# Queueing the S5 powers and matrices on VectorE behind the row norm of the second half of c

## The chip, the cores and the metric

The kernel runs on one core of a Trainium2 chip. The core has five engines that run side by side, each with its own queue that is worked through in order: TensorE (PE in the profile: matrix products and transposes), VectorE (DVE), ScalarE (ACT), GpSimd (POOL) and SyncE (SP, which issues the transfers here). An instruction that waits for another engine holds up all that is queued behind it on its own engine. The metric is the device time of one execution in microseconds (us).

## The reference

One layer on 1024 tokens of width 1024, all in float32: a layer norm, then a mixer of two branches, then a cross-attention and an MLP, each with its own residual and layer norm. The change lies in the first part of the mixer:

```python
z = h @ w_in                       # u 256 | c_q 256 | c_kv 256 | k_r 32 | gate 2048
y = s5_ssm(u, ...)                 # a diagonal complex state space, 16 groups of 64 states
q = rms_norm(c_q, q_norm_g) @ w_uq
kv = rms_norm(c_kv, kv_norm_g) @ w_ukv
```

`s5_ssm` forms a step factor a = exp(lam * dt) for every state, a factor f, and the scaled input matrix f * b; then it scans h(t) = a h(t-1) + b u(t) along the tokens and reads out with c. `rms_norm` divides each row of 256 by its root mean square.

## The kernel before, in words

**Tiles.** Token t of the input is c * 8 + s with s from 0 to 7; a tile of 128 rows holds one s. h0, the normed input, is kept feature-major as a pair of tiles, a rounded high part and a remainder; every large product is three TensorE passes (`mm3`, L147 to L152): high times high, high times low, low times high. Weights are split in the same way by `split_w` (L110 to L123): a transfer, a ScalarE cast (L120) and a GpSimd subtraction (L122).

**c.** `c_gemm(hf)` (L580 to L611) computes c_q and c_kv side by side for four row tiles (one half of the tokens) into two double PSUM banks. ScalarE copies the four results out (L596) and forms the sums of squares of each half row (L600). VectorE scales them and adds the epsilon (L602); `rsqrt` (L163 to L167) takes a VectorE reciprocal (L163), a ScalarE square root (L164), and three VectorE steps that refine it (L165 to L167). Then the rows are scaled: c_q by ScalarE (L610), c_kv by VectorE (L608). `c_T(hf, tl, ks)` turns one 128-column block k of the four tiles: `to_feature` has four TensorE transposes (L232) into a PSUM bank, the reading of that bank by ScalarE (L242) or, for the odd k, by VectorE too (L240), and a subtraction (L245) on VectorE, or on GpSimd for k = 2. The half 0 is computed first (`ct0`), the half 1 (`ct1`) has the four turns of half 0 as filling between its products.

**u.** The loop at L689 computes u and k_r for each s (24 passes of 288 columns into a PSUM bank), which ScalarE copies out (L699), and VectorE the 32 columns of k_r (L701). Before s = 3, 4, 5 and 6 one turn of ct1 is done.

**S5 on VectorE.** Between ct0 and ct1 stands the S5 preparation: the tables of sine and cosine and the exponentials (`exp_small`, `sincos`, L434 to L499), and then, from L649, the powers 0 to 8 of the step factor (L651 to L654, and three rounds of complex products in `cmul`, L503 to L508, at L671), the factor f (L656 to L668) and the scaled input matrix (L680). All of these are small: 8 to 128 columns. Behind the u loop stand the matrices of eight steps: G (L714 to L719) and O (L721 to L726), each 1024 columns wide, and the negated c (L728).

**What follows.** `gs_gemm(0)` and `gs_gemm(1)` (L733 to L741) are two long gate products; then TensorE turns G (L749) and takes the small products of G with c (L759, L760) between the passes of `gs_gemm(2)`. VectorE adds the skip (L772), turns k_r by its angles (L796 to L799), and the scan begins (from L831). O is first read at L887.

**Order.** The text of the kernel is not the order of the queues. A planner takes all instructions with their dependencies, plays the program through with costs of its own, and fills each engine's queue; of the instructions that are ready for an engine, the one that was written first goes first. So the place in the text acts as a priority, and something written far below can go ahead when nothing written above it is ready by the planner's clock. PSUM has four single banks (tag `ps1`) and two double ones here; the "x" tiles that hold c, u, G and O are eight.

## Time and profile before

| | us |
|---|---|
| median of 3 runs | 1653.34 |
| lowest and highest | 1650.19 and 1653.36 |
| profiled execution | 1652.23 |
| its span in the trace | 1650.4 |
| TensorE busy | 1539.5 (93%) |
| VectorE busy | 1243.3 (75%) |
| ScalarE busy | 976.5 (59%) |
| GpSimd busy | 988.0 (60%) |

The profile shows one execution. In a view in order of time each row has the start, the duration, the engine, the line of the kernel, the operation, the tiles it writes and reads with their shapes, the count, and in square brackets how long the engine was idle before it and what released it. Rows of neighbours overlap by some 0.07 us, since one instruction starts while the last is draining. In a view of waits each row has who waited for whom, the total, the count and the longest. In a view by windows the columns are the window, its length, the busy time (and instructions) of PE, PE's weight loads, DVE, ACT and POOL, the mean granted TensorE clock (1.00 is full), the share of the transfer engines, and GB/s.

### The profile page before, as it was taken

Reading aid. Unit: us, or ns where it says so; the run is one execution under the profiler, and the core shown is the slowest. Engines: PE = TensorE matmul, PEld = TensorE weight load, DVE = VectorE, ACT = ScalarE, POOL = GpSimd, SP = SyncE. Lnnn points to the kernel's source line nnn. Section 1 sums busy time; section 2 is a strip of 40 time slices with the busy share of each in tenths; the row PEclk is TensorE's granted clock in tenths of the full one; section 3 lists DMA queues with packets and bytes.
Section 4 is the critical chain, followed back from the end, with each engine's and each line's share of the span. In section 5 each row is a group of like instructions: output and inputs, shape, how many; then the busy total and the mean of one; then the engine's idle time right before and its main releaser. Section 6 shows DMA issues by size and latency. Waiting matters only on the chain.

```text
span 1650.4 us, 20758 instructions
## 1 busy us (share of the span) xinstructions
PE 1539.5 (93%) x7480; PEld 1263.0 (77%) x7480; DVE 1243.3 (75%) x1977; ACT 976.5 (59%) x1415; POOL 988.0 (60%) x538
## 2 busy tenths in 40 slices
PE   6979999999989999999977899899999999999995
PEld 4867778778768778778866687678888888888884
DVE  7970926767777969956574686999598949876998
ACT  5632235666678537684573647766866766667661
POOL 3223243664547767665563554676878767878776
PEclk9989999999999999999998899999999999999998
DMA  6212121111052541103220120022111302021102
GB/s 240 81 39 71 53 71 56 59 60 50 15 177 81 201 154 51 52 0 129 102 102 1 32 86 37 28 75 64 39 51 52 102 1 77 26 103 50 57 22 102
DMA packets 40107, 117.61 MB, mean 71 GB/s; under 512 B 4804, under 2 KB 6340, under 8 KB 40004
## 3 DMA queue, kind: packets, MB, share of 16 engines
q1 hardware_dynamic: 40004, 116.29, 20.5%
q8 instruction: 59, 0.97, 0.2%
q14 instruction: 44, 0.36, 0.1%
HBM read 98.90 MB, written 16.78 MB: 70 GB/s over the span
## 4 chain that ended last, share of the span: by engine, by line
PE 71%; DVE 15%; ACT 7%; POOL 3%; issue 3%; DMA 1%; SPq 0%; POOLq 0%; ACTq 0%; DVEq 0%
PE b L151 20%; PE b L150 20%; PE b L152 20%; DVE sx L1192 1%; PE bb L1034 1%; PE b L1071 1%; DVE c L182 1%; DVE t L371 1%; PE bb L1037 1%; DVE sx L1223 1%; ACT bb L367 1%; PE bb L1038 1%; PE b L1090 1%; DVE sx L224 1%; DVE sa L1249 1%
## 5 line engine op out<-in xcount | busy, mean ns | idle before, releaser
L151 PE MATMUL b<-sw,sa 128*128 128x512 f32 (+3 forms) x1504 | 579.6, 385 | 12.8 <-POOL sw L375 6.7
L150 PE MATMUL b<-sw,sa 128*128 128x512 f32 (+3 forms) x1504 | 578.6, 385 | 12.8 <-ACT sw L120 5.4
L152 PE MATMUL b<-sw,sa 128*128 128x512 f32 (+3 forms) x1504 | 577.7, 384 | 2.7 <-POOL sa L375 2.2
L151 PEld LDWEIGHTS b<-sw,sa 128*128 128x128 f32 x1504 | 284.7, 189 | 71.8 <-POOL sw L375 10.3
L150 PEld LDWEIGHTS b<-sw,sa 128*128 128x128 f32 x1504 | 284.5, 189 | 69.2 <-ACT sw L120 5.7
L152 PEld LDWEIGHTS b<-sw,sa 128*128 128x128 f32 x1504 | 284.5, 189 | 57.9 <-POOL sa L375 4.0
L375 POOL TENSOR_TENSOR sa<-t,sa 128x1024 fp32r<-128x1024 f32 x105 | 257.6, 2469 | 118.8 <-ACT sa L373 106.9
L367 ACT COPY bb<-sa 128x1024 f32<-128x1024 f32 x230 | 233.1, 1018 | 135.8 <-DVE t L371 69.1
L1192 DVE TENSOR_TENSOR sx<-sx,b 128x512 f32<-128x512 f32 x288 | 185.1, 675 | 35.2 <-PE b L152 35.0
L375 POOL TENSOR_TENSOR sw<-t,sw 128x1024 fp32r<-128x1024 f32 x73 | 180.9, 2484 | 43.4 <-ACT sw L373 34.2
L371 DVE TENSOR_TENSOR t<-bb,sa 128x1024 f32<-128x1024 f32 x119 | 144.1, 1217 | 35.1 <-ACT bb L367 18.9
L1249 DVE TENSOR_TENSOR sa<-sa,b 128x512 f32<-128x512 f32 x192 | 124.9, 678 | 46.8 <-ACT sa L1247 33.7
L373 ACT CAST sa<-t 128x1024 fp32r<-128x1024 f32 x105 | 109.1, 1049 | 59.3 <-DVE t L371 58.9
L362 POOL TENSOR_TENSOR sa<-sa,sa 128x1024 fp32r<-128x1024 f32 x36 | 90.2, 2519 | 57.8 <-ACT sa L361 34.2
L122 POOL TENSOR_TENSOR sw<-sraw,sw 128x1024 fp32r<-128x1024 f32 (+4 forms) x28 | 61.9, 2219 | 87.4 <-ACT sw L120 81.8
L150 PE MATMUL b<-sa,sw 128*128 128x512 f32 (+1 forms) x272 | 101.5, 373 | 3.3 <-DVE sa L1249 3.3
L152 PE MATMUL b<-sa,sw 128*128 128x512 f32 (+1 forms) x272 | 99.2, 365 | 0.0
L151 PE MATMUL b<-sa,sw 128*128 128x512 f32 (+1 forms) x272 | 99.2, 365 | 0.0
L362 POOL TENSOR_TENSOR sw<-sa,sw 128x1024 fp32r<-128x1024 f32 x32 | 81.1, 2550 | 27.9 <-ACT sw L361 27.9
L371 DVE TENSOR_TENSOR t<-bb,sraw 128x1024 f32<-128x1024 f32 x53 | 64.2, 1217 | 33.8 <-POOL sw L375 17.8
L373 ACT CAST sw<-t 128x1024 fp32r<-128x1024 f32 x73 | 76.2, 1052 | 15.3 <-PE b L151 7.6
L375 DVE TENSOR_TENSOR sw<-bb,sw 128x1024 fp32r<-128x1024 f32 x47 | 57.2, 1217 | 5.6 <-ACT sw L373 5.5
(341 smaller groups left out, 2792.5 us busy)
## 6 DMA issues: line engine op xcount, KB each, us to landing
sa<-in_w_up_dram SPq DMA_DIRECT2D x24, 512.0 KB, 4.0
sa<-in_w_dn_dram SPq DMA_DIRECT2D x24, 512.0 KB, 4.3
sx<-in_x_dram SPq DMA_DIRECT2D x16, 512.0 KB, 5.8
d_h<-t SPq DMA_DIRECT2D x16, 256.0 KB, 2.3
sraw<-in_w_gs_dram SPq DMA_DIRECT2D x8, 512.0 KB, 3.2
d_gs<-t SPq DMA_DIRECT2D x16, 256.0 KB, 2.9
t<-d_gs SPq DMA_DIRECT2D x16, 256.0 KB, 2.8
d_ms<-t SPq DMA_DIRECT2D x16, 256.0 KB, 2.1
```

The costliest lines, as they stand in the source:

```text
L122: (nc.vector if self.rawtag == "a" and self.nsw % SWV == 0 else nc.gpsimd).tensor_sub(lo[:, :cols].bitcast(FR), raw[:, :cols], hi[:, :cols])
L150: mm(out, A[0].bitcast(FR), B[0].bitcast(FR), start=start, stop=False)
L151: mm(out, A[0].bitcast(FR), B[1].bitcast(FR), start=False, stop=False)
L152: mm(out, A[1].bitcast(FR), B[0].bitcast(FR), start=False, stop=stop)
L182: self.nc.vector.bn_stats(st[:, h, :], x[:, h * 512:(h + 1) * 512])
L362: (GP if z is x[c] else V).tensor_sub(H[c][1].bitcast(FR), z, H[c][0])
L367: A.copy(P[c], x[c])
L371: V.tensor_tensor(T[c], P[c], y[c], op=op)
L373: A.copy(H[c][0].bitcast(FR), T[c])
L375: (V if T[c] is P[c] else GP).tensor_sub(H[c][1].bitcast(FR), T[c], H[c][0])
L1192: V.tensor_tensor(v, v, b, op=op)
L1249: V.tensor_tensor(z[:, s_], z[:, s_], b, op=op)
```

## The change

The text of `ct1 = c_gemm(1, ...)` and of the whole u loop is moved up: ahead of the powers instead of behind the scaled input matrix. `c_gemm` keeps the last of its VectorE row scalings (L608) in `k_.last_ts`. And all that stands from the powers to the negated c is put into a block, `tc.issue_after(ct1_last)`, which gives each VectorE instruction of the block an edge to that last scaling: the planner may queue it only behind it. The edge is one of order in VectorE's queue; it adds no wait between engines. Instructions of other engines, and VectorE's sine, cosine and exponentials ahead of the block, get no edge. The order in which tiles are asked for stays the same.

```diff
@@ c_gemm
-                    V.tensor_scalar(z, z, y[:, 2 * t + i:2 * t + i + 1], None, op0=ALU.mult)
+                    k_.last_ts = V.tensor_scalar(z, z, y[:, 2 * t + i:2 * t + i + 1], None, op0=ALU.mult)
@@ body, behind sincos
+    ct1 = c_gemm(1, [lambda k=k: c_T(0, ct0, (k,)) for k in range(4)])
+    ct1_last = k_.last_ts.ins
+    Uc = [k_.slot("x"), k_.slot("x")]
+    krx = k_.slot("x")
+    V.memset(krx[:, 0:768], 0.0)
...
+    for s in range(8):
+        if 2 < s < 7:
+            c_T(1, ct1, (s - 3,))
...
+        V.tensor_copy(krw[:, s, :], b[:, 256:288])
+
+    g_ = tc.issue_after(ct1_last)
+    g_.__enter__()
 
     apr = s5t(9)
     api = s5t(9)
...
     k_.cmul(V, bbr, bbi, frb, fib, br, bi, bt_)
-    ct1 = c_gemm(1, [lambda k=k: c_T(0, ct0, (k,)) for k in range(4)])
-    Uc = [k_.slot("x"), k_.slot("x")]
...
-        V.tensor_copy(krw[:, s, :], b[:, 256:288])
-
     Or, Oi, Gr, Gi = (k_.slot("x") for _ in range(4))
...
     V.tensor_scalar(nci, ci, -1.0, None, op0=ALU.mult)
+    g_.__exit__(None, None, None)
```

## The prediction

> **What bounds the kernel now.** I read first the page's busy shares and its chain of work that ended last, then the list of what TensorE waited for, then the order of time on TensorE, ScalarE and VectorE around one of its longest waits.

> ```profile
> PE 1539.5 (93%) x7480; PEld 1263.0 (77%) x7480; DVE 1243.3 (75%) x1977; ACT 976.5 (59%) x1415; POOL 988.0 (60%) x538
> PE 71%; DVE 15%; ACT 7%; POOL 3%; issue 3%; DMA 1%; SPq 0%; POOLq 0%; ACTq 0%; DVEq 0%
> ...
> PE b L150 <- ACT sa L1411: 11.8, 4, 7.1
> ...
> PE b L232 <- ACT sx L610: 10.2, 1, 10.2
> ...
> PE b L150 <- ACT sw L361: 4.1, 1, 4.1
> ```

> TensorE is the bound: it is idle for 1650.4 - 1539.5 = 110.9 us in all. 10.2 us of that are one wait, for the scaling L610 of c, and this is the place that the change is about. TensorE's order of time there:

> ```profile
> 83.67 0.29 PE L152 MATMUL b<-sw,sa 128*128 128x288 f32 x1
> 94.22 1.67 PE L232 MATMUL b<-cst,sx 128*128 128x128 f32 x4 [10.25 <-ACT sx L610]
> 95.54 0.59 PE L150 MATMUL b<-sw,sa 128*128 128x288 f32 x1
> 95.93 0.44 PE L151 MATMUL b<-sw,sa 128*128 128x288 f32 x1
> ...
> 100.01 0.34 PE L150 MATMUL b<-sw,sa 128*128 128x288 f32 x1
> ```

> TensorE has done three of the eight u products (83.97), then wants to transpose the normed second half of c, gets it at 94.22 and comes to the fourth u product at 95.54: 11.57 us later than its own queue would have had it, transposes included. ScalarE and VectorE say why:

> ```profile
> 80.48 0.19 ACT L600 ACTIVATION_READ_ACCUMULATOR t<-sx 128x1 f32 x1
> 80.87 1.06 ACT L120 CAST sw<-sraw 128x1024 fp32r<-128x1024 f32 x1
> 90.97 0.21 ACT L164 ACTIVATE c<-c 128x8 f32<-128x8 f32 x1 [9.04 <-DVE c L163]
> 93.65 1.71 ACT L610 ACTIVATE sx<-sx,c 128x256 f32<-128x256 f32 x4 [2.15 <-DVE c L167]
> ```

> ```profile
> 77.99 0.43 DVE L497 TENSOR_TENSOR sa<-sa,sx 128x264 f32<-128x264 f32 x1
> 78.41 1.25 DVE L245 TENSOR_TENSOR sa<-t,sa 128x512 fp32r<-128x512 f32 x1
> 82.10 2.38 DVE L508 TENSOR_TENSOR sa<-sa,sx 128x16 f32<-128x16 f32 x1
> 84.40 0.21 DVE L955 TENSOR_SCALAR sa<-sa 128x128 f32<-128x128 f32 x1
> 85.04 0.74 DVE L240 TENSOR_SCALAR t<-b,c 128x512 f32<-128x512 f32 x1
> 86.11 1.07 DVE L245 TENSOR_TENSOR sa<-t,sa 128x512 fp32r<-128x512 f32 x1
> 88.42 0.70 DVE L686 MEMSET sx<- 128x768 f32 x1
> 89.55 0.16 DVE L602 TENSOR_SCALAR c<-c 128x8 f32<-128x8 f32 x1
> 89.62 1.21 DVE L714 TENSOR_TENSOR sx<-sa,sx 128x1024 f32<-128x1024 f32 x1
> 93.45 0.17 DVE L167 SCALAR_TENSOR_TENSOR c<-c,c 128x8 f32<-128x8 f32 x1
> 94.67 1.13 DVE L608 TENSOR_SCALAR sx<-sx,c 128x256 f32<-128x256 f32 x4
> ```

> The sums of squares are in at 80.67. The next step of the norm, L602 on VectorE, starts at 89.55, because VectorE's queue has S5 work ahead of it. From L602 to L610 it is another 93.65 - 89.55 = 4.10 us for five tiny VectorE steps (L602, L163, L165 to L167) and a tiny one of ScalarE (L164), because a 1024-column S5 product (L714 and the like, 1.21 us) stands between each two.

> **The change part by part.** (a) The work moved behind L608 is 41 small operations (L651 to L680), twelve 1024-column ones (L714 to L726) and L728; all are VectorE's, and no DMA and no other engine's instruction moves. What stays ahead of L602 once TensorE's half is in: sine and cosine up to L497 (78.42), then those that are ahead of it today and don't belong to S5: L245 1.25, L240 0.74, L245 1.07, L686 0.70 and L955 twice 0.21, some 4.2 us less their small overlaps. So L602 could start at about 82.1, by 7.4 us sooner. The earliest is 80.75, when the squares are in, if the planner lets L602 pass them.

> (b) From L602 to L610 without the S5 products: the six tiny steps are some 0.17 us each (L602 0.16, L164 0.21, L167 0.17) with a hand-over between, for which I take 1.5 us in place of 4.10. Bounds: 1.0 (their bare durations, with nothing between) and 4.1 (other copies slip between).

> (c) A collision comes with it. The 16-column L508 above took 2.38 us, where L508 on 32 columns takes 0.18; it ended with a GpSimd subtraction that began just before it:

> ```profile
> 82.06 2.38 POOL L122 TENSOR_TENSOR sw<-sraw,sw 128x1024 fp32r<-128x1024 f32 x1 [10.16 <-ACT sw L120]
> 86.01 0.18 DVE L508 TENSOR_TENSOR sa<-sa,sx 128x32 f32<-128x32 f32 x1
> ```

> Today an S5 operation waits there; after the change it is the norm, or what stands just ahead of it, that is held until 84.44. With L602 or L163 held, L610 comes at 82.1 + 1.5 + 2.1 = 85.7; without the collision at 83.6. I take 85.7, since the norm's steps lie in the middle of that subtraction. [...]

> L610 at 85.7 in place of 93.65 is 7.95 us. TensorE's transposes and the fourth u product hang on L610 by 0.57 and 1.89 us, so that product starts at 87.6, and TensorE still idles some 2.3 us behind 83.97.

> (d) The clock. After the gap the u products start 0.24 us apart (95.93 to 100.01 in 17 steps); the granted clock in windows:

> ```profile
> 84.00:86.00 2.00, 0.00 (x0) 0.00 (x0) 2.00 (x9) 0.00 (x0) 0.45 (x1) 1.00 0.26 63
> 86.00:88.00 2.00, 0.00 (x0) 0.00 (x0) 2.00 (x4) 0.00 (x0) 0.00 (x0) 0.61 0.53 199
> 98.00:100.00 2.00, 2.00 (x10) 2.00 (x9) 1.87 (x2) 0.00 (x0) 0.00 (x0) 0.50 0.00 0
> 102.00:104.00 2.00, 2.00 (x17) 2.00 (x17) 1.19 (x2) 0.74 (x1) 0.00 (x0) 1.00 0.00 0
> 164.00:166.00 2.00, 0.31 (x4) 0.10 (x3) 1.95 (x7) 0.99 (x3) 1.47 (x2) 1.00 0.00 0
> 490.00:492.00 2.00, 2.00 (x6) 1.52 (x6) 1.72 (x2) 1.63 (x3) 0.00 (x0) 0.50 0.98 346
> ```

> At the half clock half of the 95.93 to 100.01 is lost, 2.0 us. The clock fell within 2.5 us of the start of the gap (it is 0.61 over 86 to 88); after the wait of 4.1 us for L361, at 488, it stands at 0.50 too, and it held around 165, where TensorE was idle for most of two us. A remaining gap of 2.3 us lies between, so I count 1.5 us of the 2.0 as gained; the bounds are 0 and 2.0. [...]

> (e) What the moved work costs in its new place. Its cover is TensorE's way from the fourth u product to the transposes L749 of the matrices G, its first reader:

> ```profile
> 114.89 0.40 PE L150 MATMUL b<-sa,sw 128*128 128x512 f32 x1
> 136.70 2.26 PE L749 MATMUL b<-cst,sx 128*128 128x128 f32 x16
> ...
> 95.90:119.00 23.10, 23.10 (x150) 22.37 (x150) 15.82 (x18) 10.03 (x18) 6.49 (x3) 0.91 0.02 4
> 119.00:160.00 41.00, 40.86 (x198) 30.98 (x196) 0.45 (x1) 9.15 (x13) 14.12 (x11) 1.00 0.28 95
> ```

> TensorE idles 0.14 us from 95.9 to 160, while VectorE is busy for 16.3 of those 64 us. After the change L749 would come at about 136.7 - 9.5 = 127. VectorE starts on S5 at about 87; G needs the small operations (78.42 to 88.42 today, less the 6.7 us of L245 twice, L240, L955, one 1.21 product and the hold of L508 that lie between: 3.3 us, and I add one for L651 to L659, of which some run earlier today), six products of 1.21 (7.3 us) and what comes between of L245, L240 and L701 (1.07, 0.74 and 0.18 each; some 4 us): ready at about 103, 24 us early. So the later S5 costs nothing; without that cover it would cost what it is late at L749. What follows to 160 is TensorE's own dense work and moves forward as it is.

> **Sum**, against the profiled execution's 1652.23 us (span 1650.4): 7.95 + 1.5 = 9.45, so 1642.8. The median of the runs shown, 1653.34, is 1.1 above that execution; I keep to the execution. Bounds: L602 at 80.75, 1.0 to L610 and no collision put L610 at 81.75, which is 11.9 sooner, with the clock's 2.0 13.9 in all, 1638.3; L602 held to 84.6 and 4.1 us to L610 (88.7) and a clock that falls all the same make 4.95 and 1647.3.

> **Rivals.** *Given back later*: each engine's queue is filled by a planner, so that another order at 85 us may deal out other orders behind; the late waits of TensorE (L1411 above, 11.8 us in four) hang on ScalarE's turn, not on VectorE's at 85 us. For it: nothing fixes that order. Against: what TensorE reads first from the moved part has 24 us to spare, so no plan has cause to change. It would give 1648 to 1655, with 1651 as its middle.

> *Slower: the copies that free the PSUM banks are stuck.* A u product and its transposes take two of the four banks, and VectorE's L240, L245 and L701 must read them before the next but one can start. If the planner queues these behind the whole S5 block, TensorE stops two steps on. A step is 3.63 us:

> ```profile
> 101.01 0.44 PE b L232 x4
> 104.64 0.44 PE b L232 x4
> ...
> 95.72 0.18 DVE L701 COPY sx<-b 128x32 f32<-128x32 f32 x1
> ```

> TensorE would stop at 87.6 + 7.3 = 95 and go on when the block (4 + 12 products of 1.2, with L726 up to 3.3: 20 us) and two us of copies are through, at 109; three steps of 3.63 then end at 120, against 114.89 for the start of the gate product today. With another cold start of 2 us it is 7 us slower: 1659. It decides from where the copies stand more than 7.3 us behind their banks, and turns into a loss from some 17 us. Against it: VectorE takes an L701 at 95.72 today, between two products, and the change writes them ahead of S5.

> *More than the sum*: the norm misses the GpSimd subtraction and passes L245 and L686: below 1638.3, 1638 say. For it: the planner already runs L955, written far below, ahead of S5. Against: it puts all these ahead of L602 today.

> *It doesn't do what it says*: the planner fills the freed place with other VectorE work and L602 stays at 89: 1652. Against: no other such work is ready, by VectorE's 0.45 us between 119 and 160.

> **How the numbers follow.** Likeliest (1638.3 to 1647.3) 0.62; more than the sum 0.07; given back 0.20, of which 0.09 still count as faster; stuck banks 0.09; not what it says 0.02. A difference of under 0.2% (3.3 us) can't be told from none here. Faster: 0.62 + 0.07 + 0.09 = 0.78; same 0.11 + 0.02 = 0.13; slower 0.09. The range 1637.5 to 1651 leaves out the half of "more", the upper half of "given back" that is not faster, and the stuck banks.

> **What would show it.** Right: TensorE's wait for L610 falls from 10.2 to between 0 and 4 us; L602 runs at 81 to 85 with no 1024-column operation before L608; the fourth u product starts at 86 to 89; L749 comes 8 to 12 us earlier and waits for nothing. Wrong: a wait of TensorE on L240, L245 or L701 between 90 and 125; L749 waiting for VectorE; L602 still past 88; or all this as said, and waits behind 250 us that grow by as much.

## The result and the profile after

The change takes 1644.21 us (median of 4 runs, 1643.22 to 1644.69) against 1653.01 us of the kernel before on the same chip (4 runs, 1650.19 to 1653.36): a ratio of 0.9949, 95% interval 0.9936 to 0.9961, or 8.8 us faster. The profiled execution took 1644.69 us, its span is 1642.9. In a second set of runs, as the control `e10_change_again` below, it was 1643.07 against 1652.87, ratio 0.9947 (0.9935 to 0.996).

Lines behind L602 have moved: the copies of the u loop are L667 and L669 now (L699 and L701 before), the memset L686 is L654, the transposes of G are L753 (L749).

The page's busy shares, and what TensorE waited for over the whole span (who waited for whom: total, count, longest):

```profile
PE 1539.7 (94%) x7480; PEld 1263.2 (77%) x7480; DVE 1249.7 (76%) x1977; ACT 977.1 (59%) x1415; POOL 989.8 (60%) x538
...
PE b L150 <- ACT sa L1415: 11.8, 4, 7.1
...
PE b L232 <- ACT sx L610: 2.0, 1, 2.0
```

TensorE does the same work in the same time (1539.7 against 1539.5 us busy); its wait for the row scaling L610 fell from 10.2 to 2.0 us, and the late waits for ScalarE (11.8 in four) stand as they were. Its order of time around the place, in the changed kernel:

```profile
85.95 1.52 PE L232 MATMUL b<-cst,sx 128*128 128x128 f32 x4 [2.05 <-ACT sx L610]
87.23 0.38 PE L150 MATMUL b<-sw,sa 128*128 128x288 f32 x1
...
106.07 0.40 PE L150 MATMUL b<-sa,sw 128*128 128x512 f32 x1
...
127.87 2.27 PE L753 MATMUL b<-cst,sx 128*128 128x128 f32 x16
```

The fourth u product starts at 87.23 (95.54 before), the first gate product at 106.07 (114.89), and the transposes of G at 127.87 (136.70) without a wait. Of the 8.82 us at the gate product, 95.54 - 87.23 = 8.31 are the wait; the other 0.51 are a little more full clock on the way from there (114.89 - 95.54 = 19.35 us before, of which 4.56 at the half clock, 95.54 to 100.10; 106.07 - 87.23 = 18.84 now, of which 3.41, 87.70 to 91.11). VectorE and GpSimd of the changed kernel show the rest of the norm:

```profile
78.24 1.22 DVE L245 TENSOR_TENSOR sa<-t,sa 128x512 fp32r<-128x512 f32 x1
79.35 0.37 DVE L959 TENSOR_SCALAR sa<-sa 128x128 f32<-128x128 f32 x2
79.62 0.76 DVE L240 TENSOR_SCALAR t<-b,c 128x512 f32<-128x512 f32 x1
80.42 1.29 DVE L245 TENSOR_TENSOR sa<-t,sa 128x512 fp32r<-128x512 f32 x1
81.81 0.70 DVE L654 MEMSET sx<- 128x768 f32 x1
82.41 1.86 DVE L602 TENSOR_SCALAR c<-c 128x8 f32<-128x8 f32 x1
...
85.39 1.14 DVE L608 TENSOR_SCALAR sx<-sx,c 128x256 f32<-128x256 f32 x4
...
101.10 1.21 DVE L722 TENSOR_TENSOR sx<-sx,sa 128x1024 f32<-128x1024 f32 x1
```

```profile
81.86 2.39 POOL L122 TENSOR_TENSOR sw<-sraw,sw 128x1024 fp32r<-128x1024 f32 x1 [10.02 <-ACT sw L120]
```

Ahead of L602 stand the operations that the prediction listed; L602 starts at 82.41, is held for 1.86 us, and ends with the GpSimd subtraction at 84.25. From then it is 1.1 us to the scaling: L610 starts with L608 at 85.39. The last product of G, L722, ends at 102.31, 25.6 us before TensorE turns G.

The granted clock of the changed kernel by windows (window, its length, PE, PE's weight loads, DVE, ACT, POOL, clock, share of the transfer engines, GB/s):

```profile
84.28:87.70 3.42, 1.54 (x7) 0.97 (x8) 3.08 (x27) 2.52 (x10) 0.00 (x0) 1.00 0.46 153
87.70:91.11 3.41, 3.41 (x17) 3.41 (x16) 3.41 (x28) 1.57 (x3) 0.00 (x0) 0.50 0.00 0
...
418.79:422.20 3.41, 1.82 (x13) 1.22 (x12) 3.12 (x5) 2.95 (x6) 2.65 (x3) 1.00 0.00 0
422.20:425.60 3.40, 3.40 (x15) 2.82 (x14) 2.09 (x4) 1.12 (x3) 0.00 (x0) 0.50 0.01 2
463.20:466.60 3.40, 3.40 (x16) 3.22 (x16) 1.09 (x3) 1.17 (x2) 1.04 (x1) 0.50 0.93 329
```

The clock still falls behind the short gap, from 87.70 to 91.11. The last three rows are of places far from the change. Ahead of 422.20 TensorE was busy for 1.82 of 3.41 us, and then the clock is half; the kernel before was at the full clock in these places:

```profile
431.00:434.40 3.40, 3.40 (x26) 2.92 (x25) 3.17 (x6) 1.93 (x5) 0.00 (x0) 1.00 0.01 5
469.50:472.90 3.40, 2.76 (x20) 2.28 (x20) 1.94 (x5) 1.69 (x4) 1.57 (x2) 1.00 0.90 280
```

In these two places the profiled execution gives back some of its gain. Two of TensorE's waits, one ahead of them and one behind, show it: the wait for VectorE's t, and the one for L361. In the kernel before:

```profile
396.10 0.39 PE L150 MATMUL b<-sw,sa 128*128 128x256 f32 x1 [0.30 <-DVE t L1098]
...
488.33 0.96 PE L150 MATMUL b<-sw,sa 128*128 128x512 f32 x3 [4.06 <-ACT sw L361]
```

and after:

```profile
387.66 0.39 PE L150 MATMUL b<-sw,sa 128*128 128x256 f32 x1 [0.30 <-DVE t L1102]
...
482.40 0.97 PE L150 MATMUL b<-sw,sa 128*128 128x512 f32 x3 [4.06 <-ACT sw L361]
```

The lead is 8.44 us at the first and 5.93 at the second. At the end it is 1652.23 - 1644.69 = 7.54. Between 855 and 935 us the kernel before has nine windows of 3.41 us at the half clock, with 17.37 us of TensorE's work, and this execution eight, with 13.67; half of the difference, 1.85 us, is about the 1.61 by which the lead grows again.

### The profile page after: what moved, and what is told of

Read it like the earlier page. It is cut to its first block, busy times and chain, and to the rows that moved or that the text cites. A ratio compares the mean times of both kernels' runs of the same rounds, so it can differ in the third digit from the quotient of the medians.

```text
span 1642.9 us, 20758 instructions
## 1 busy us (share of the span) xinstructions
PE 1539.7 (94%) x7480; PEld 1263.2 (77%) x7480; DVE 1249.7 (76%) x1977; ACT 977.1 (59%) x1415; POOL 989.8 (60%) x538
## 5 line engine op out<-in xcount | busy, mean ns | idle before, releaser
L151 PE MATMUL b<-sw,sa 128*128 128x512 f32 (+3 forms) x1504 | 579.0, 385 | 13.0 <-POOL sw L375 6.8
L150 PE MATMUL b<-sw,sa 128*128 128x512 f32 (+3 forms) x1504 | 577.7, 385 | 12.8 <-ACT sw L120 5.5
L152 PE MATMUL b<-sw,sa 128*128 128x512 f32 (+3 forms) x1504 | 577.1, 384 | 2.5 <-POOL sa L375 2.2
L151 PEld LDWEIGHTS b<-sw,sa 128*128 128x128 f32 x1504 | 284.1, 189 | 71.7 <-POOL sw L375 10.5
L150 PEld LDWEIGHTS b<-sw,sa 128*128 128x128 f32 x1504 | 284.0, 189 | 68.8 <-ACT sw L120 5.7
L152 PEld LDWEIGHTS b<-sw,sa 128*128 128x128 f32 x1504 | 284.1, 189 | 57.9 <-POOL sa L375 4.1
L122 POOL TENSOR_TENSOR sw<-sraw,sw 128x1024 fp32r<-128x1024 f32 (+4 forms) x28 | 61.9, 2219 | 86.0 <-ACT sw L120 77.2
L150 PE MATMUL b<-sa,sw 128*128 128x512 f32 (+1 forms) x272 | 101.5, 373 | 3.2 <-DVE sa L1253 3.2
L152 PE MATMUL b<-sa,sw 128*128 128x512 f32 (+1 forms) x272 | 99.2, 365 | 0.0
L151 PE MATMUL b<-sa,sw 128*128 128x512 f32 (+1 forms) x272 | 99.2, 365 | 0.0
```

What stands on the lines that cost most here:

```text
L122: (nc.vector if self.rawtag == "a" and self.nsw % SWV == 0 else nc.gpsimd).tensor_sub(lo[:, :cols].bitcast(FR), raw[:, :cols], hi[:, :cols])
L150: mm(out, A[0].bitcast(FR), B[0].bitcast(FR), start=start, stop=False)
L151: mm(out, A[0].bitcast(FR), B[1].bitcast(FR), start=False, stop=False)
L152: mm(out, A[1].bitcast(FR), B[0].bitcast(FR), start=False, stop=stop)
```

## The experiments

All ran against the kernel before on the same chip; the order of TensorE's instructions is that of the kernel before in each, but for the added ones. Inserted lines shift the line numbers by up to three from those of the changed kernel.

**1. Is it the text or the edge?** The change without the edge: the text is moved, nothing else.

```diff
-    g_ = tc.issue_after(ct1_last)
-    g_.__enter__()
...
-    g_.__exit__(None, None, None)
```

> The text is moved up as in the change, but there is no edge from the S5 block to the last row scaling. If the edge is what counts (the planner takes S5 work because it is ready sooner, whatever its place in the text), L602 stays at 88 to 90 us, TensorE waits some 10 us for L610 and the time is that of before, 1652 to 1654. If the place in the text is what counts, L602 comes at 82 to 84 and the time is that of the change, 1643 to 1645.

1652.5 us (11 runs) against 1652.73: ratio 0.9999 (0.999 to 1.0008). In its trace, VectorE and TensorE:

```profile
89.23 0.17 DVE L602 TENSOR_SCALAR c<-c 128x8 f32<-128x8 f32 x1
...
93.91 1.28 PE L232 MATMUL b<-cst,sx 128*128 128x128 f32 x3 [10.33 <-ACT sx L610]
```

The norm is as late as before. A place higher up in the text does nothing here by itself; with the same text, the edge makes the difference. (The edge without the moved text was run for the products alone, in the next experiment.)

**2. The products alone.** The text of before, and the edge only on the twelve 1024-column products and the negated c; the powers stay ahead of the norm.

```diff
+    ct1_last = k_.last_ts.ins
...
+    g_ = tc.issue_after(ct1_last)
+    g_.__enter__()
...
+    g_.__exit__(None, None, None)
```

> The text stays as before; only the twelve 1024-column products and the negated c get the edge, the powers, the factor and the input matrix stay ahead of the row norm. By the sum of the prediction this takes away the products between L602 and L610 (4.10 us before, 1.5 expected) and the one product that stands ahead of L602 (1.2), and leaves the rest of the queue ahead of L602: L602 at 87 to 88.5, L610 at 89 to 90, a gain of 3.5 to 5 us, 1648 to 1649.5. If the powers are the whole delay, nothing is gained (1653); if the products are, all of it (1644).

1648.89 us against 1652.73: ratio 0.9979 (0.997 to 0.9988). VectorE and TensorE:

```profile
88.30 0.15 DVE L602 TENSOR_SCALAR c<-c 128x8 f32<-128x8 f32 x1
...
89.57 0.62 DVE L608 TENSOR_SCALAR sx<-sx,c 128x256 f32<-128x256 f32 x2
...
91.46 0.59 PE L150 MATMUL b<-sw,sa 128*128 128x288 f32 x1
```

L602 is 1.25 us sooner, one product less ahead of it, and from L602 to the scaling (L610 starts with L608, at 89.57) it is 1.27 us in place of 4.10. The fourth u product comes 4.08 us sooner. So of the change's 8.31 us about half is the products; the rest is, by difference, the small operations (powers, factor, input matrix).

**3. What did the cold clock cost?** The kernel before, with 40 matmuls of 512 columns in the gap of TensorE, whose results nobody reads (added work).

```diff
+        if s == 3:
+            jb = k_.bank2()
+            for j in range(40):
+                PE.matmul(jb[:, 0:512], ..., start=j == 0, stop=j == 39)
         if 2 < s < 7:
             c_T(1, ct1, (s - 3,))
```

> The kernel before, with 40 matrix products of 512 columns whose result nobody reads put on TensorE into the gap ahead of the first turn of ct1 (work is added, none taken away). At 0.227 us each they fill 9.1 of the 10.25 us. If the half clock behind the gap is a cost of its own and comes of the idling, the clock stays full, the u products behind it start 0.133 us apart in place of 0.24, and the first gate product starts 1.5 to 2.0 us sooner: 1651 to 1651.5. If the idling does not matter for the clock, or the clock not for the products, the time is 1653; if the added work is in the way, it is longer.

1650.22 us against 1652.73: ratio 0.999 (0.9982 to 0.9999). TensorE's order of time:

```profile
83.63 9.27 PE L693 MATMUL bb<-sa,sa 128*128 128x512 f32 x40
...
95.45 0.38 PE L150 MATMUL b<-sw,sa 128*128 128x288 f32 x1
...
112.77 0.40 PE L150 MATMUL b<-sa,sw 128*128 128x512 f32 x1
```

The norm is as late as before (95.45 for the fourth u product against 95.54), yet the gate product comes at 112.77: 17.32 us of way in place of 19.35. The half clock behind the gap costs 2.03 us by itself, as the prediction read off. Over the whole time the medians differ by 2.5 us, with an interval from 0.2 to 3.0; 1651 to 1651.5 were expected.

**4. Without the collision, by GpSimd's order.** The change, with the GpSimd subtraction that met L602 (and all GpSimd work of that gate product) queued behind a later GpSimd subtraction of c, the L245 of the turn k = 2 (`k_.last_gp`).

```diff
-    gs_gemm(0)
+    with tc.issue_after(k_.last_gp.ins):
+        gs_gemm(0)
```

> The change, and in addition GpSimd's subtraction for the first gate weight (the L122 that begins at 81.86) is queued behind its subtraction for the third turn of c, some 18 us later; its reader comes at 106. If that subtraction holds L602 for the length that L602 takes there (1.86 in place of 0.16 us), L602 ends 1.7 us sooner, L610 comes at 83.6 to 83.8, TensorE idles under 0.5 us, the clock does not fall there and the first gate product starts 2 to 3.5 us sooner than with the change: 1641 to 1643 in all. If the long L602 has another cause, L610 stays at 85.4 and the time at 1644.

1646.34 us against 1652.73: ratio 0.9963 (0.995 to 0.9975). That misses the 1641 to 1643 that were expected; it isn't shown to be less than the change's gain either, whose interval (0.9936 to 0.9961) overlaps. TensorE, VectorE and GpSimd:

```profile
85.55 0.38 PE L150 MATMUL b<-sw,sa 128*128 128x288 f32 x1
...
106.46 0.50 PE L150 MATMUL b<-sa,sw 128*128 128x512 f32 x1 [2.93 <-DVE sx L671]
```

```profile
96.72 2.64 DVE L723 TENSOR_TENSOR sa<-sa,sx 128x1024 f32<-128x1024 f32 x1
99.28 2.37 DVE L854 COPY sa<-sa 128x8 f32<-128x8 f32 x1
```

```profile
98.24 3.38 POOL L122 TENSOR_TENSOR sw<-sraw,sw 128x1024 fp32r<-128x1024 f32 x1
```

The norm does gain what the collision took: the fourth u product comes at 85.55, 1.68 us sooner than in the change. But GpSimd's work now runs between 94.9 and 105.1 with hardly a break, and meets the S5 work there. A product takes 2.64 us (1.21 elsewhere), an 8-column copy 2.37 (0.16) and, from 102.78, an 8-column product 2.31, so the copy L671 that frees a PSUM bank is late, and TensorE waits 2.93 us for it: the gate product comes at 106.46, 0.39 later than in the change. This is the prediction's "stuck copies", on a small scale.

**5. Without the collision, by ScalarE's order.** The cast of that weight, on ScalarE, is queued behind the last of the row scalings L610 (`k_.last_ml`) instead, so that the GpSimd subtraction comes behind the norm.

```diff
-    gs_gemm(0)
+    with tc.issue_after(k_.last_ml.ins):
+        gs_gemm(0)
```

> The change, and ScalarE's cast of the first gate weight (L120 at 80.67) is queued behind its row scalings L610, so that GpSimd's subtraction comes at about 86.5 and meets small S5 operations in place of the norm. If the subtraction is what holds L602, L610 comes at 83.5 to 83.9 and TensorE comes to the fourth u product with under 0.6 us of idling and a full clock: 11 to 12 us sooner than before. Theory of the stuck copies: VectorE's S5 work starts only 0.7 us later than in the change but TensorE 3 us sooner, so a copy that frees a PSUM bank (L669) may come late by 0 to 2 us around 100 to 110; 1641 to 1643 in all. Theory that only the weight was late in the run without the collision (GpSimd's subtraction 17 us later there): no wait at all around 103, 1640.5 to 1641.5.

1645.4 us against 1652.75: ratio 0.9964 (0.995 to 0.9978). Both theories of the expectation had it lower, at 1640.5 to 1643. VectorE and TensorE:

```profile
84.45 1.53 PE L232 MATMUL b<-cst,sx 128*128 128x128 f32 x4 [0.30 <-ACT sx L610]
...
87.03 2.41 DVE L504 TENSOR_TENSOR sx<-sa 128x16 f32<-128x16 f32 x1
...
91.66 0.40 PE L150 MATMUL b<-sw,sa 128*128 128x288 f32 x1 [2.06 <-DVE sx L669]
...
107.06 0.40 PE L150 MATMUL b<-sa,sw 128*128 128x512 f32 x1
```

The collision has only moved: a 16-column S5 operation is held from 87.03, the powers behind it are late, and with them the bank's copy. TensorE's wait for L610 falls from 2.05 to 0.30 us and returns as 2.06 us for L669. Two more waits for that copy follow, of 0.93 us at 96.47 and 0.23 at 100.59, so that the gate product comes at 107.06, 0.99 later than in the change.

**6. The same with a late O.** The six products of O queued behind the last k_r copy as well.

> As the run with the cast behind the norm, and in addition the six products of O (first read at 200 us) are queued behind the last copy of k_r. By the theory of the stuck copies VectorE then keeps up with TensorE from 90 to 106 us, no copy is late, and TensorE has no wait over 0.5 us between 84 and 150: the fourth gate stage starts 11.5 to 12 us sooner than before and the time is 1640.5 to 1642. If the copies are not the cause, it equals the run without the late O within 0.5 us.

1644.46 us against 1652.75: ratio 0.9955 (0.9942 to 0.9968). The two later waits of experiment 5, 1.16 us in all, are gone; that much of the expectation came. The rest of it missed: the first wait stands at 91.94, ahead of any O product, and the gate product still comes only at 107.26. That wait, and the windows around it:

```profile
91.94 0.44 PE L150 MATMUL b<-sw,sa 128*128 128x288 f32 x1 [2.06 <-DVE sx L669]
```

```profile
88.76:92.17 3.41, 1.35 (x11) 1.11 (x10) 3.41 (x19) 1.95 (x4) 0.94 (x1) 1.00 0.42 145
92.17:95.58 3.41, 3.41 (x16) 3.41 (x16) 3.41 (x4) 0.00 (x0) 0.00 (x0) 0.50 0.02 8
```

Around the wait of experiment 5:

```profile
87.16:90.58 3.42, 2.43 (x20) 2.19 (x18) 3.42 (x10) 3.03 (x6) 2.25 (x1) 1.00 0.02 4
90.58:93.99 3.41, 2.33 (x17) 2.33 (x18) 3.41 (x12) 0.23 (x1) 0.00 (x0) 1.00 0.41 150
```

Behind one and the same wait of 2.06 us the clock is half here (0.50 from 92.17) and full there (it stays at 1.00 behind 93.99 too). Equal gaps do not make equal clocks. The windows are cut where each execution's own clock edges lie, a whole number of 3.413 us apart. By them the wait here lies within one window, which leaves TensorE 1.35 us of work in it; there an edge at 90.58 cuts the wait, and both windows keep over 2.3.

**7. How much cover has the moved block?** The change, with the whole S5 block queued behind the last k_r copy (the end of the u loop) instead of the last row scaling.

```diff
-        V.tensor_copy(krw[:, s, :], b[:, 256:288])
+        kr_last = V.tensor_copy(krw[:, s, :], b[:, 256:288])
-    g_ = tc.issue_after(ct1_last)
+    g_ = tc.issue_after(kr_last.ins)
```

> The change with the whole S5 block behind the last copy of k_r (some 20 us later than in the change) in place of the last row scaling. The prediction says that G has 24 us of cover ahead of TensorE's transposes of it: S5 starts at about 106, G is ready at 119 to 127, TensorE transposes it at 128: no cost, 1643 to 1645. If there is less cover than that, TensorE waits for VectorE there and the time grows by that wait, up to 1650.

1643.51 us against 1652.75: ratio 0.9947 (0.9935 to 0.996), the change's own. The last product of G and TensorE's turn:

```profile
126.99 1.21 DVE L722 TENSOR_TENSOR sx<-sx,sa 128x1024 f32<-128x1024 f32 x1
...
128.35 0.85 PE L753 MATMUL b<-cst,sx 128*128 128x128 f32 x6 [0.19 <-DVE sa L506]
```

G is done 25.9 us later than in the change, and TensorE waits 0.19 us. The cover was 25.6 us and it is now used up.

**8. And beyond the cover.** The same with G's six products done three times (twelve more, each giving the same values).

> As the late block, and the six products of G are done three times (twelve products of 1.21 us are added, 14.5 us on VectorE). The cover is then gone: G is ready at 133 to 142 and TensorE waits 6 to 14 us for it, with a cold clock behind the wait: 1651 to 1660. If something else sets that stage's end, the time stays at 1644 to 1646.

1661.77 us against 1652.75: ratio 1.0058 (1.0045 to 1.0072). The longest of TensorE's waits between 75 and 250:

```profile
PE b L754 <- DVE sx L720: 15.3, 1, 15.3
```

With the cover gone, all twelve products of 1.21 us (14.5 us) appear as a wait of 15.3, and the time is 18.3 us above experiment 7, more than was expected on both counts. Behind the wait, from 143.28 to 149.4, TensorE is slower, as at the half clock: eight transposes take 1.94 us, twice (sixteen take 2.27 in the change), and two 512-column products start 0.42 us apart (0.23 ahead of the wait). This is the likely place of the other 3 us. That the moved work costs nothing in the change is its cover, not its nature.

**9. Both cures together.** The cast behind the norm (5), the block behind the last k_r copy (7), and O behind G's last product: no S5 work is left near the GpSimd subtraction or the copies.

> Both cures together: the cast of the first gate weight behind the row scalings (so GpSimd does not hold the norm), and the S5 block behind the last copy of k_r (so the held S5 operations do not stand ahead of the copies that free PSUM banks), with the products of O behind those of G so that G is ready by 122 to 124. If the late copies (2.1 us) were all that kept the earlier norm from paying, the first gate stage starts 11.5 to 12 us sooner than before, against 8.8 with the change and 9.4 with the late block, and the time is 1640.5 to 1642. If G is late, TensorE waits for it at about 125 and the time is that of the change, 1644. Two or three us either way can come from where the clock's windows fall later.

1642.32 us (5 runs, 1638.59 to 1643.7) against 1652.87: ratio 0.9935 (0.9921 to 0.9949). Its VectorE and TensorE:

```profile
82.73 0.11 DVE L602 TENSOR_SCALAR c<-c 128x8 f32<-128x8 f32 x1
...
84.52 1.52 PE L232 MATMUL b<-cst,sx 128*128 128x128 f32 x4 [0.33 <-ACT sx L610]
85.80 0.38 PE L150 MATMUL b<-sw,sa 128*128 128x288 f32 x1
...
103.12 0.40 PE L150 MATMUL b<-sa,sw 128*128 128x512 f32 x1
```

The norm is free, the way to the gate product is 17.32 us, that of the full clock in experiment 3, and the product comes 11.77 us sooner than in the kernel before. Of this the profiled execution kept 8.53 at its end (1652.23 - 1643.70). Its median is the lowest of all, though 0.3 us above the 1640.5 to 1642 that were expected, but its interval overlaps that of the change (0.9935 to 0.996 in the control, which shared its runs of the kernel before), so that it beats the change isn't shown.

**10. The change again, as a control**, in the same runs as 9.

> The change itself once more, on the same chip and beside the same runs of before as the combined kernel: 1643 to 1646. If the gain of 8.8 us held only on the first chip, it comes out elsewhere.

1643.07 us against 1652.87. The same kernel, the same order of TensorE's instructions, and another clock far behind the change:

```profile
422.20:425.60 3.40, 3.40 (x26) 2.92 (x25) 3.18 (x6) 1.93 (x5) 0.00 (x0) 1.00 0.02 5
461.80:465.20 3.40, 3.40 (x16) 2.95 (x15) 1.73 (x3) 2.00 (x4) 1.07 (x2) 0.50 0.89 263
```

```profile
387.30 0.39 PE L150 MATMUL b<-sw,sa 128*128 128x256 f32 x1 [0.30 <-DVE t L1102]
...
480.02 1.65 PE L150 MATMUL b<-sw,sa 128*128 128x512 f32 x3 [4.06 <-ACT sw L361]
```

At 422 the clock is full here and half in the first profile; at 462 it is half in both. The lead is 8.80 us at the first wait and 8.31 at the second, where the first profile had 8.44 and 5.93. So the 2.5 us given back belong to the execution and not to the queues' order. Ahead of that place TensorE was busy for 2.00 of the 3.41 us up to the window's edge here (417.40 to 420.81), and for 2.01 in the kernel before (427.78 to 431.19), against 1.82 in the first profile: another cut of the same gap.

## Why the prediction was right, point by point

It said 1642.8 with 1637.5 to 1651.0 around it; 1644.21 was measured. Against the execution it argued from, it promised 9.45 us, and the profiled execution has 7.54. The 1.9 us between split into three: (a) to (c) gave 0.36 more than was counted, (d) 0.99 less, and 1.28 of the 8.82 at the gate product were given back by the end.

**(a) L602** was put at 82.1 and came at 82.41, behind exactly the operations that were named.

**(b) From L602 to L610** 1.5 us were taken for the bare chain; experiment 2, which has no hold there, measured 1.27. That a product stood "between each two" of the steps before is not quite what the trace shows: three stood between L602 and L166 (L714, L716 and L717), and only a copy ahead of L167. The sum doesn't use it.

**(c) The collision** went as taken: L602 was held until the GpSimd subtraction ended, and L610 came at 85.39 where 85.7 was said. L602 took 1.86 us here against 0.11 in experiment 9. What (a) to (c) give together, 8.31 us, was put at 7.95.

**(d) The clock** is the term that was mis-sized. All of the 2.0 us were there to gain (2.03 in experiment 3, and in 9), I counted 1.5, and the change got 0.51: behind its gap of 2.05 us the clock fell all the same, for about 3.4 us. I had placed 2.3 us between a wait of some two us that kept the clock and one of 4.1 that lost it, and leaned to the better side. Experiments 5 and 6 show one wait of 2.06 us that keeps the clock and one that loses it, so a length alone decides nothing in this range. The gap is also more than its wait: from 83.9 to 87.2 TensorE does only four transposes, and it was busy for 1.54 of the 3.42 us ahead of 87.70.

**(e) The cover** held. G was said to be ready at about 103 and was at 102.3; L753 was said to come at 127 and came at 127.87, with no wait. The 24 us of cover that were worked out are 25.6, and experiments 7 and 8 spent it and then overspent it.

**Of the rivals**, "it doesn't do what it says" describes experiment 1 to the letter (L602 at 89.23, 1652.5 us), but not the change. "Stuck copies" didn't come in the change and did, at 2 to 3 us and not at the 14 that were reckoned (95 to 109), in experiments 4, 5 and 6, as soon as GpSimd's subtractions met the S5 work. "More than the sum" asked for the norm to miss the GpSimd subtraction; experiment 9 built that and had 11.77 us at the gate product, though its median, 1642.32, is not below 1638.3. "Given back later" came in part and by another cause: TensorE's queue has the same order from end to end, but the clock fell in other places. That took 2.5 us in the profiled execution (8.44 to 5.93; the end stands at 7.54) and 0.5 in the control.

Why the clock falls at 422 in one execution and not in the next can be read in part. The low stretches in the traces of the kernel before and of the change, but the one in each that the end of the kernel cuts off, are one or several times 3.413 us long, and within an execution their edges stand at whole multiples of 3.413 us from each other. Cut at these edges, the two traces have, between 40 and 1600 us, 7 windows at the full clock in which TensorE was busy for less than 30%: a half one follows each. They have 862 with more than 62%, and a half one follows none. Of the 17 between, 5 are followed by a half one. So an idle time counts by how it lies against the windows, and when the work shifts against them the clock can fall in other places. What decides between 30% and 62% stays open: in the change 1.82 us of work stood ahead of the fall at 422, and 1.51 in the window from 476.82 to 480.23, which no fall followed. No run set the windows, so that they are the cause rests on this agreement alone.

## What to carry to other kernels

When TensorE waits for a short chain on a busy VectorE, list what is queued ahead of the chain and between its steps, and find out how far off the first reader of each is: work with 25 us of cover can go behind the chain for nothing, and only an edge, not a place in the text, may make the planner do it. Before moving an operation away from a collision, look at what the freed engine meets next: here the same 2 us moved twice (experiments 4 and 5) and were gone at the gate product only when both neighbours had been moved (experiment 9). A gain at one place of a long kernel arrives at its end give or take some 3 us (here 7.54 of 8.82 in the change, 8.53 of 11.77 in experiment 9), because the clock falls in other places from one execution to the next (at 422 us in one execution of the change, not in another); measure it at a nearby instruction too, as the gate product is used here.
